# A recurrent unit's last tile worked by token halves, with one pair of weight buffers opened ahead of the unit and two high parts made by casting transfers

## The chip, the cores and the metric

The kernel runs on one core of one Trainium2 chip. The metric is the device time in microseconds (us) of one execution. The engines are named as in the profile: PE (TensorE, matrix products), DVE (VectorE), ACT (ScalarE), POOL (GpSimd) and SP (SyncE, which issues transfers). PEld is PE's loading of weights, which overlaps PE.

## The reference, cut to what matters

The program is one step of a two-layer model on 640 tokens (512 latent tokens, then 128 context tokens) of width 1024. Layer 0 is an attention layer with its feed-forward part; layer 1 is a bidirectional gated recurrent unit, then a feed-forward part. The change touches the end of layer 1's recurrent unit and the projection behind it:

```python
a = jnp.exp(log_a)
b = jnp.sqrt(-jnp.expm1(2.0 * log_a)) * (i * xc)
def step(h, ab):            # one scan per direction, forward and backward
    a_t, b_t = ab
    h = a_t * h + b_t
    return h, h
y = (hs_f + hs_b) * jax.nn.gelu(gate)
return y @ w_out, jnp.stack([hT_f, hT_b], axis=1)
# then, with one gate value per channel:
x = x + g * (y @ w_out)
# and the RMS norm of x, the modulation and the feed-forward part
```

The latent scans start from given states, the context scans from zero; the final context states are an output of their own.

## The kernel before

All data lie with the channels on the 128 partitions, in 8 tiles of channels, and the tokens along the free dimension. Every product in fp32 is made of three matmuls of rounded operands: each operand is split into a high part (a cast) and a low part (the operand minus its high part), and hi·hi, hi·lo and lo·hi are added in PSUM. So a matrix operand is not ready for PE until its cast is done, and not wholly until its subtraction is done too.

**The recurrent unit** (`lru_xr`, `lru_a`, `lru_b`, `lru_c`, `lru_gate`, `lru_d`) runs over the 8 channel tiles f, one behind the other with overlap. For each tile ACT makes sigmoids, an exponential and a square root (L1316 to L1321), DVE multiplies by the root (L1322), makes four scans (L1330: two directions, latent 512 and context 128 columns), copies the final states (L1332), adds both directions in the grid's order (L1337, L1338), multiplies by the gate (L1343), and the result y is split by L1348 (ACT, high) and L1350 (DVE, low). For the last tile, 7, the last two steps go in the two token halves of 320, (0, 320) and (320, 640).

**The projection** (`project_halves`) multiplies y (8 tiles k) by `w_out`, in 8 units f of 128 output channels, each for two token halves c0 and c1; every pair of unit and half is 24 matmuls of 320 columns, in a PSUM buffer of its own (three under the name "mm", three under "mx"). Five of them, f0c0, f0c1, f1c0, f1c1 and f2c0, start early: with k = 0 to 4, and then in turns with k = 5, 6 and 7, as the tiles of y come in. Between the turns k = 6 and k = 7 stand ten small dummy products (`keep`, L211; PE's records show twenty). Then follow f3 to f7 of c0, the sum of squares over channels of c0 (`stat`: matmuls L551 and L554, a variance on DVE L556, a power on POOL L558, a diagonal on DVE L560 and its broadcast by PE, L568), f2 to f7 of c1, and the same sum of squares for c1. A finished PSUM buffer is evicted by DVE (L598, a multiply-add on x, in two pieces where latent and context tokens meet), ACT squares the row, DVE adds the square (L537), and x goes to DRAM. The feed-forward part follows (L1168 to L1170 are its first three groups' matmuls, L1130 its product of gate and up).

**The weights** of a unit come by a transfer into `raw` (three buffers), are cast by ACT (L181) and subtracted by DVE (L183). The pairs are called whi/wlo (three buffers) or whx/wlx (three, opened with the feed-forward part's pool).

**The order.** Each engine runs its own list of instructions in order. The lists are written by a planner at build time, which runs a model of the machine; program code fixes a place only where it pins an instruction behind another (`issue_after`). So a change at one place may reorder others.

## Time and profile before

| | us |
|---|---|
| median of 3 runs (1506.61 to 1507.72) | 1506.66 |
| the profiled execution | 1508.43 |
| its span (first to last instruction) | 1506.4 |
| PE busy | 1483.1 (98%) |
| DVE busy | 1063.1 (71%) |
| ACT busy | 701.6 (47%) |
| POOL busy | 222.5 (15%) |

The busy shares are means over stages of different limits. The recurrent unit lies before about 1011 us of the span, its projection until about 1057, then the feed-forward part.

### The profile page before, as it was taken

The numbers are of one execution on the slowest core, as the hardware profiler recorded it, in microseconds if no ns is written. First come the engines' busy times: TensorE is split into PE (matmuls) and PEld (weight loads), VectorE is DVE, ScalarE is ACT, GpSimd is POOL, SyncE is SP. The second block draws the span as 40 slices with busy tenths as digits, with TensorE's granted clock in tenths as the row PEclk, the third lists the DMA queues.
The fourth block names the chain that finished last, engine by engine and source line by source line (L and its number), as shares of the span: only waits on it lengthen the run. The fifth ranks groups of instructions, "written<-read, shape, count | busy, mean of one in ns | idle before, by whom it ended". The sixth has DMA issues, their size and how long they took to land. (4 is left out here: it accounts for less than half of the span.)

```text
span 1506.4 us, 26172 instructions
## 1 busy us (share of the span) xinstructions
PE 1483.1 (98%) x10409; PEld 1435.1 (95%) x10409; DVE 1063.1 (71%) x2015; ACT 701.6 (47%) x1271; POOL 222.5 (15%) x260
## 2 busy tenths in 40 slices
PE   8999999999999999999999999999999999999997
PEld 6999999899999999999999988899999999999997
DVE  5778998679999997444443778986975665655555
ACT  4576766664332123312321569884634342524243
POOL 0112132101111110000000100000331323232311
PEclk9999999999999999999999999999999999999999
DMA  9644766446566664222222544325233131313221
GB/s 377 174 146 159 188 189 174 119 144 193 182 183 197 208 198 133 62 84 84 65 65 92 148 142 127 106 90 186 103 113 98 57 113 57 112 57 103 66 57 71
DMA packets 72330, 196.66 MB, mean 131 GB/s; under 512 B 8048, under 2 KB 24592, under 8 KB 72080
## 3 DMA queue, kind: packets, MB, share of 16 engines
q1 hardware_dynamic: 57392, 142.32, 29.9%
q0 software_dynamic: 14240, 51.98, 11.4%
q8 instruction: 82, 1.34, 0.4%
q10 hardware_dynamic: 576, 0.68, 0.1%
q14 instruction: 40, 0.33, 0.1%
HBM read 179.48 MB, written 8.92 MB: 125 GB/s over the span
## 5 line engine op out<-in xcount | busy, mean ns | idle before, releaser
L229 PE MATMUL mm<-big,whi 128*128 128x320 f32 (+3 forms) x1224 | 380.3, 311 | 1.1 <-DVE big L1350 0.9
L228 PE MATMUL mm<-big,whi 128*128 128x320 f32 (+3 forms) x1224 | 378.6, 311 | 1.5 <-ACT big L574 0.6
L230 PE MATMUL mm<-big,wlo 128*128 128x320 f32 (+3 forms) x1224 | 378.0, 310 | 0.2 <-DVE wlo L183 0.2
L228 PEld LDWEIGHTS mm<-big,whi 128*128 128x128 f32 x1224 | 229.8, 188 | 3.7 <-ACT big L574 0.9
L229 PEld LDWEIGHTS mm<-big,whi 128*128 128x128 f32 x1224 | 230.1, 188 | 3.2 <-DVE big L1350 1.5
L230 PEld LDWEIGHTS mm<-big,wlo 128*128 128x128 f32 x1224 | 230.5, 188 | 1.6 <-DVE wlo L183 0.5
L257 DVE SCALAR_TENSOR_TENSOR mprod<-mraw,csb 128x1024 f32<-128x1024 f32 x160 | 195.1, 1220 | 11.4 <-DMA mraw<-in_wm 11.0
L598 DVE SCALAR_TENSOR_TENSOR x<-mm,G,x 128x320 f32<-128x320 f32 (+2 forms) x192 | 77.7, 435 | 80.4 <-PE mm L230 80.2
L181 ACT CAST whi<-raw 128x1024 fp32r<-128x1024 f32 (+1 forms) x71 | 73.8, 1040 | 109.5 <-PE mm L229 63.4
L183 DVE TENSOR_TENSOR wlo<-raw,whi 128x1024 fp32r<-128x1024 f32 (+1 forms) x87 | 105.2, 1209 | 24.7 <-ACT whi L181 11.9
L229 PE MATMUL mm<-big,whx 128*128 128x320 f32 (+3 forms) x348 | 108.2, 311 | 0.0
L230 PE MATMUL mm<-big,wlx 128*128 128x320 f32 (+3 forms) x348 | 107.7, 310 | 0.0
L228 PE MATMUL mm<-big,whx 128*128 128x320 f32 (+3 forms) x348 | 107.6, 309 | 0.0
L253 POOL DMA_DIRECT2D mraw<-in_wm x80 | 43.1, 539 | 355.2 <-DVE mprod L257 272.2
L229 PE MATMUL mx<-big,whi 128*128 128x320 f32 (+3 forms) x281 | 87.0, 309 | 0.0
L230 PE MATMUL mx<-big,wlo 128*128 128x320 f32 (+3 forms) x281 | 86.8, 309 | 0.0
L228 PE MATMUL mx<-big,whi 128*128 128x320 f32 (+3 forms) x281 | 86.7, 309 | 0.0
L181 ACT CAST whx<-raw 128x1024 fp32r<-128x1024 f32 (+1 forms) x40 | 41.1, 1029 | 84.6 <-PE mm L229 45.7
L230 PE MATMUL mx<-big,wlx 128*128 128x320 f32 (+3 forms) x260 | 80.5, 309 | 0.0
L229 PE MATMUL mx<-big,whx 128*128 128x320 f32 (+3 forms) x260 | 80.4, 309 | 0.0
L228 PE MATMUL mx<-big,whx 128*128 128x320 f32 (+3 forms) x260 | 80.1, 308 | 0.0
L1348 ACT CAST whi<-raw 128x1024 fp32r<-128x1024 f32 (+1 forms) x41 | 41.3, 1007 | 73.2 <-PE mm L229 44.5
(363 smaller groups left out, 3710.4 us busy)
## 6 DMA issues: line engine op xcount, KB each, us to landing
raw<-in_gu SPq DMA_DIRECT2D x88, 512.0 KB, 3.5
mraw<-in_wm POOLq DMA_DIRECT2D x80, 512.0 KB, 4.0
raw<-in_dn SPq DMA_DIRECT2D x24, 512.0 KB, 3.7
sw<-in_wm SPq DMA_DIRECT2D x16, 512.0 KB, 10.7
raw<-in_wqk SPq DMA_DIRECT2D x16, 512.0 KB, 5.0
raw<-in_wi SPq DMA_DIRECT2D x16, 512.0 KB, 3.5
whi<-in_wi POOLq DMA_DIRECT2D x16, 512.0 KB, 3.9
raw<-in_dn SPq DMA_DIRECT2D x16, 448.0 KB, 3.3
```

What stands on the lines that cost most here:

```text
L181: nc.scalar.copy(hi, raw)
L183: nc.vector.tensor_tensor(lo, raw, hi.bitcast(F32), ALU.subtract)
L228: nc.tensor.matmul(ps, hi[:, k], xhi[:, k, s], start=(k == 0), stop=False)
L229: nc.tensor.matmul(ps, hi[:, k], xlo[:, k, s], start=False, stop=False)
L230: self.done = nc.tensor.matmul(ps, lo[:, k], xhi[:, k, s], start=False, stop=(k == last)).ins
L253: nc.gpsimd.dma_start(w, self.i["wm"][l * 6 + j - 2, f])
L257: nc.vector.scalar_tensor_tensor(prod, w, 1.0, self.csb[:, s], ALU.mult, ALU.mult, accum_out=out[:, s, f:f + 1])
L598: self.nc.vector.scalar_tensor_tensor(xs, ps[:, a - t0:b - t0], G[:, s, f:f + 1], xs, ALU.mult, ALU.add)
L1348: self.nc.scalar.copy(hi, v)
```

## The change

1. For tile 7 the recurrent unit's last multiply (L1322 before) is left to a new function `lru_end`, which works by parts in a written, pinned order: the latent columns' multiply, their two scans, the sums up to token 320, the gate and cast of half c0, and only then the context columns, their scans, and half c1. The copy of the final states comes last.
2. The high parts of tiles 5 and 6 are made by a casting transfer on POOL's queue, not by a cast of ACT.
3. Unit f2 of the projection takes a whx/wlx pair from a new pool `wp` that is opened ahead of the recurrent unit; its high part and that of unit f3 come by casting transfers from DRAM. So f2's low part can be made before the unit ends.
4. The turn k = 7 is divided by halves: first c0, with matmuls of f3 put between, then c1. The dummies go. f3's three parts run as all hi·hi, all hi·lo, all lo·hi.
5. The eviction of a half of the k = 7 turn is pinned behind the last subtraction of weights, and the transfer of the final states moves behind the projection in the code.

```diff
-    def unit(self, src, slot=None, after=None, nx=3):
+    def unit(self, src, slot=None, after=None, nx=3, cast=False):
...
-        if self.ptags == ["at"]:
-            nc.gpsimd.dma_start(hi, src)
+        if cast or self.ptags == ["at"]:
+            with self.pin(self.cast if after else None):
+                nc.gpsimd.dma_start(hi, src)
         else:
             nc.scalar.copy(hi, raw)
-        with self.tc.issue_after(after) if after else nullcontext():
-            nc.vector.tensor_tensor(lo, raw, hi.bitcast(F32), ALU.subtract)
+        with self.pin(after):
+            self.low = nc.vector.tensor_tensor(lo, raw, hi.bitcast(F32), ALU.subtract).ins
         return hi, lo
+
+    def wxs(self, shape, n=3):
+        if self.wp is None:
+            return [self.t(shape, F32R, v, n, self.sb) for v in ("whx", "wlx")]
+        self.nx += 1
+        n, pool = (1, self.wp) if self.nx % 3 == 1 else (2, self.sb)
+        return [self.t(shape, F32R, v, n, pool) for v in ("whx", "wlx")]
...
-        us = [self.unit(w[f], "m") for f in range(3)]
+        us = [self.unit(w[f], "mmx"[f], cast=f == 2) for f in range(3)]
...
-        turns = sorted(zip(early, pss), key=lambda e: e[0][1])
-        for k in range(KT - 3, KT):
-            if k == KT - 1:
-                self.keep(self.ps("at"), 10)
+        def turn(k, turns, pin=None):
             for (f, t0, t1), ps in turns:
                 for part in us[f]:
-                    self.done = self.nc.tensor.matmul(ps, part[:, k], hi[:, k, t0:t1], start=False, stop=False).ins
+                    with self.pin(pin):
+                        pin = self.done = self.nc.tensor.matmul(ps, part[:, k], hi[:, k, t0:t1], start=False, stop=False).ins
             for (f, t0, t1), ps in turns:
                 self.done = self.nc.tensor.matmul(ps, us[f][0][:, k], lo[:, k, t0:t1], start=False, stop=(k == KT - 1)).ins
                 if k == KT - 1:
-                    out(f, t0, t1, ps)
-        for f in range(3, KT):
-            us.append(self.unit(w[f], "mx"[f % 2]))
-            out(f, *CH[0], self.chunk(us[f], hi, lo, *CH[0]))
+                    with self.pin(self.low):
+                        out(f, t0, t1, ps)
+        sides = [[e for e in zip(early, pss) if e[0][1:] == c] for c in CH]
+        for k in range(KT - 3, KT - 1):
+            turn(k, sides[0] + sides[1])
+        us.append(self.unit(w[3], "m", ended, cast=True))
+        turn(KT - 1, sides[0])
+        t0, t1 = CH[0]
+        ps = self.ps("mx")[:, 0:HT]
+        for j, (part, v) in enumerate(((0, hi), (0, lo), (1, hi))):
+            if j == 2:
+                turn(KT - 1, sides[1], self.done)
+            for k in range(KT):
+                self.done = self.nc.tensor.matmul(ps, us[3][part][:, k], v[:, k, t0:t1], start=(j == k == 0),
+                                                  stop=(j == 2 and k == KT - 1)).ins
+        out(3, t0, t1, ps)
+        for f in range(4, KT):
+            us.append(self.unit(w[f], "xm"[f % 2]))
+            out(f, *CH[0], self.chunk(us[f], hi, lo, *CH[0], pins={0: self.done} if f == 4 else {}))
...
     def lru_d(self, f, y, G, yhi, ylo):
-        for a, b in CH if f == KT - 1 else ((0, NTOK),):
-            self.nc.vector.tensor_tensor(y[:, a:b], y[:, a:b], G[:, a:b], ALU.mult)
-            self.split(yhi[:, f, a:b], ylo[:, f, a:b], y[:, a:b])
+        self.nc.vector.tensor_tensor(y, y, G, ALU.mult)
+        hi, lo = yhi[:, f, 0:NTOK], ylo[:, f, 0:NTOK]
+        if f < KT - 3:
+            self.split(hi, lo, y)
+            return
+        self.cast = self.nc.gpsimd.dma_start(hi, y).ins
+        self.nc.vector.tensor_tensor(lo, y, hi.bitcast(F32), ALU.subtract)
+
+    def lru_end(self, f, a, h, root, G, yhi, ylo):
...
+        rooted(0)
+        for d in range(2):
+            dve(self.scan, f, a, h, d, 0)
+        for piece in ((56, 64, 0), (0, 32, 64)):
+            dve(self.directions, y, h, *piece)
+        gated(*CH[0])
+        rooted(1)
+        dve(self.scan, f, a, h, 0, 1)
+        low(*CH[0])
+        dve(self.scan, f, a, h, 1, 1)
+        dve(self.directions, y, h, 32, 56, 320)
+        dve(nc.vector.tensor_tensor, y[:, NLAT:NTOK], h[:, 0, C0:LW], h[:, 1, C0:LW], ALU.add)
+        gated(*CH[1])
+        low(*CH[1])
+        with self.pin(ins):
+            self.states(f, h)
+        return ins
...
+        wp = self.ctx.enter_context(tc.tile_pool(name="wp", bufs=1, reuse_waits="tile"))
         with self.phase("lru", at=1) as lp:
```

In `lru_end`, `rooted` is the multiply by the root, `directions` the sum of both directions for some columns of the grid, `gated` the multiply by the gate with ACT's cast behind it, `low` the subtraction; every DVE step is pinned behind the one before it.

**Where the order moves, first place.** DVE at the end of the recurrent unit, before (lt are the recurrent unit's tiles, gl the gate, big_9509 and big_9510 y's high and low part, st the states):

```order
L1350 TENSOR_TENSOR big_9510<-lt_10639,big_9509 128x640
L1322 TENSOR_TENSOR lt_10620<-lt_10620,lt_10619 128x1286
L1330 SCALAR_TENSOR_TENSOR lt_10620<-lt_10781,cols_61,lt_10620 128x512
L1330 SCALAR_TENSOR_TENSOR lt_10620<-lt_10781,lt_10620 128x128
L1330 SCALAR_TENSOR_TENSOR lt_10620<-lt_10781,cols_61,lt_10620 128x512
L1330 SCALAR_TENSOR_TENSOR lt_10620<-lt_10781,lt_10620 128x128
L1337 TENSOR_TENSOR lt_10781<-lt_10620 128x64
L1337 TENSOR_TENSOR lt_10781<-lt_10620 128x448
L1332 COPY st_74<-lt_10620 128x2
L1338 TENSOR_TENSOR lt_10781<-lt_10620 128x128
L1343 TENSOR_TENSOR lt_10781<-lt_10781,gl_10800 128x320 x2
L1350 TENSOR_TENSOR big_9510<-lt_10781,big_9509 128x320 x2
```

And DVE with the change, at the same place:

```order
L1380 TENSOR_TENSOR big_9510<-lt_10642,big_9509 128x640
L1390 TENSOR_TENSOR lt_10623<-lt_10623,lt_10622 128x2x512
L1351 SCALAR_TENSOR_TENSOR lt_10623<-lt_10784,cols_61,lt_10623 128x512 x2
L1356 TENSOR_TENSOR lt_10784<-lt_10623 128x64
L1356 TENSOR_TENSOR lt_10784<-lt_10623 128x256
L1390 TENSOR_TENSOR lt_10784<-lt_10784,gl_10802 128x320
L1390 TENSOR_TENSOR lt_10623<-lt_10623,lt_10622 128x2x128
L1351 SCALAR_TENSOR_TENSOR lt_10623<-lt_10784,lt_10623 128x128
L1390 TENSOR_TENSOR big_9510<-lt_10784,big_9509 128x320
L1351 SCALAR_TENSOR_TENSOR lt_10623<-lt_10784,lt_10623 128x128
L1356 TENSOR_TENSOR lt_10784<-lt_10623 128x192
L1390 TENSOR_TENSOR lt_10784<-lt_10623 128x128
```

The gate's multiply for the first half (128x320) stands behind two scans and two sums now, and behind four scans, three sums and the copy before.

PE at that place, before (mm and mx are PSUM buffers, whi/wlo and whx/wlx a unit's weights, at_11026 the dummies' buffer):

```order
L1054 MATMUL mx_10919<-big_9510,whi_10906 128x320
L211 MATMUL at_11026<-ident_63,ones_72 128x128 x10
L1052 MATMUL mm_10916<-big_9509,whi_10900 128x320
L1052 MATMUL mm_10916<-big_9509,wlo_10901 128x320
L1052 MATMUL mm_10918<-big_9509,whi_10906 128x320
L1052 MATMUL mm_10918<-big_9509,wlo_10907 128x320
L1052 MATMUL mm_10920<-big_9509,whi_10912 128x320
L1052 MATMUL mm_10920<-big_9509,wlo_10913 128x320
L1052 MATMUL mx_10917<-big_9509,whi_10900 128x320
```

And PE with the change (mx_11059 is unit f3's buffer):

```order
L1060 MATMUL mx_10923<-big_9510,whi_10910 128x320
L1075 MATMUL mx_11059<-big_9509,whi_11032 128x320 x7
L1058 MATMUL mm_10920<-big_9509,whi_10904 128x320
L1058 MATMUL mm_10920<-big_9509,wlo_10905 128x320
L1058 MATMUL mm_10922<-big_9509,whi_10910 128x320
L1058 MATMUL mm_10922<-big_9509,wlo_10911 128x320
L1058 MATMUL mm_10924<-big_9509,whx_10916 128x320
L1058 MATMUL mm_10924<-big_9509,wlx_10917 128x320
L1075 MATMUL mx_11059<-big_9509,whi_11032 128x320
L1075 MATMUL mx_11059<-big_9510,whi_11032 128x320 x7
L1060 MATMUL mm_10920<-big_9510,whi_10904 128x320
L1060 MATMUL mm_10922<-big_9510,whi_10910 128x320
```

Seven matmuls of f3 stand where the dummies stood, and eight more behind the six of half c0.

**Second place.** PE at the second sum of squares, before (mm_11547 is the first group of the feed-forward part, at_11491 the sums):

```order
L1168 MATMUL mm_11547<-big_10881,whx_11513 128x320
L1169 MATMUL mm_11547<-big_10881,whx_11513 128x320
L1170 MATMUL mm_11547<-big_10881,wlx_11514 128x320
L551 MATMUL at_11491<-ones_72,ssq_11049 128x128
L554 MATMUL at_11491<-ones_72,sq_11488 128x128
```

And with the change (mm_11454 is unit f7's second half, at_11484 the sums):

```order
L235 MATMUL mm_11454<-big_9509,whi_11215 128x320
L236 MATMUL mm_11454<-big_9510,whi_11215 128x320
L237 MATMUL mm_11454<-big_9509,wlo_11216 128x320
L558 MATMUL at_11484<-ones_72,ssq_11044 128x128
L561 MATMUL at_11484<-ones_72,sq_11481 128x128
```

Before, the 24 matmuls of the feed-forward part's first group (mm_11547) stood between f7's second half and the sums; with the change nothing stands between them, and that group comes behind the sums. Behind the six sums 15 matmuls of the next group and then the broadcast of the diagonal follow in both.

DVE there, before (x the residual stream, sq the squares, ssq their sum, big_10881 the feed-forward part's input, var and dg the variance and the diagonal):

```order
L1350 TENSOR_TENSOR big_10881<-x_10886,big_10881 128x320 x2
L598 SCALAR_TENSOR_TENSOR x_10886<-mx_11461,G_1335_7652,x_10886 128x192
L537 TENSOR_TENSOR ssq_11049<-ssq_11049,sq_11371 128x320
L598 SCALAR_TENSOR_TENSOR x_10886<-mx_11461,G_1335_7652,x_10886 128x128
L537 TENSOR_TENSOR ssq_11049<-ssq_11049,sq_11410 128x320
L537 TENSOR_TENSOR ssq_11049<-ssq_11049,sq_11449 128x320
L183 TENSOR_TENSOR wlx_11526<-raw_11523,whx_11525 128x1024
L183 TENSOR_TENSOR wlo_11532<-raw_11529,whi_11531 128x1024
L183 TENSOR_TENSOR wlx_11538<-raw_11535,whx_11537 128x1024
L556 TENSOR_SCALAR var_11498<-at_11491 128x3
L560 TENSOR_TENSOR dg_11502<-ident_63,rs_11500 128x384
```

And with the change:

```order
L605 SCALAR_TENSOR_TENSOR x_10890<-mm_11454,G_1335_7652,x_10890 128x192
L605 SCALAR_TENSOR_TENSOR x_10890<-mm_11454,G_1335_7652,x_10890 128x128
L544 TENSOR_TENSOR ssq_11044<-ssq_11044,sq_11364 128x320
L1424 TENSOR_TENSOR big_10885<-x_10890,big_10885 128x320 x3
L544 TENSOR_TENSOR ssq_11044<-ssq_11044,sq_11403 128x320
L544 TENSOR_TENSOR ssq_11044<-ssq_11044,sq_11442 128x320
L184 TENSOR_TENSOR wlx_11520<-raw_11517,whx_11519 128x1024
L184 TENSOR_TENSOR wlo_11526<-raw_11523,whi_11525 128x1024
L184 TENSOR_TENSOR wlx_11532<-raw_11529,whx_11531 128x1024
L563 TENSOR_SCALAR var_11491<-at_11484 128x3
L567 TENSOR_TENSOR dg_11495<-ident_63,rs_11493 128x384
```

Three subtractions of the feed-forward part's input (128x320) stand between the eviction and the last two additions now; the three subtractions of weights stand ahead of the variance in both.

## Rows read from the trace of the kernel before

**Rows 1.** the page, busy time: us, share of the span, instructions.

```profile
PE 1483.1 (98%) x10409; PEld 1435.1 (95%) x10409; DVE 1063.1 (71%) x2015; ACT 701.6 (47%) x1271; POOL 222.5 (15%) x260
```

**Rows 2.** the timeline of PE: start us, us, what, count, idle before and releaser.

```profile
1001.63 0.41 PE L230 MATMUL mm<-big,wlo 128*128 128x320 f32 x1 [0.21 <-DVE wlo L183]
...
1006.85 2.39 PE L211 MATMUL at<-ident,ones 128*128 128x128 f32 x20
1010.75 0.42 PE L1052 MATMUL mm<-big,whi 128*128 128x320 f32 x1 [1.51 <-ACT big L1348]
...
1016.71 0.30 PE L228 MATMUL mm<-big,whi 128*128 128x320 f32 x1
```

**Rows 3.** the timeline of DVE, the end of the recurrent unit.

```profile
998.20 0.82 DVE L1343 TENSOR_TENSOR lt<-lt,gl 128x640 f32<-128x640 f32 x1
...
1003.79 1.50 DVE L1322 TENSOR_TENSOR lt<-lt,lt 128x1286 f32<-128x1286 f32 x1 [0.35 <-ACT lt L1321]
1005.32 1.28 DVE L1330 TENSOR_TENSOR_SCAN lt<-lt,cols,lt 128x512 f32<-128x512 f32 x1
1006.52 0.40 DVE L1330 TENSOR_TENSOR_SCAN lt<-lt,lt 128x128 f32<-128x128 f32 x1
...
1008.33 1.21 DVE L1337 TENSOR_TENSOR lt<-lt 128x64 f32<-128x64 f32 x2
...
1009.69 0.92 DVE L1343 TENSOR_TENSOR lt<-lt,gl 128x320 f32<-128x320 f32 x2
...
1012.09 2.36 DVE L183 TENSOR_TENSOR wlx<-raw,whx 128x1024 fp32r<-128x1024 f32 x2 [0.46 <-ACT whx L181]
1014.71 1.01 DVE L598 SCALAR_TENSOR_TENSOR x<-mm,G,x 128x320 f32<-128x320 f32 x2 [0.26 <-issue]
```

**Rows 4.** the timeline of ACT, the same stretch.

```profile
1002.48 1.27 ACT L1321 ACTIVATE lt<-lt 128x1286 f32<-128x1286 f32 x1
...
1010.24 0.86 ACT L1348 CAST big<-lt 128x320 fp32r<-128x320 f32 x2 [4.43 <-DVE lt L1343]
```

**Rows 5.** the DMA view: tensors, queue, count, KB each, median us to landing.

```profile
whi<-in_wi POOLq DMA_DIRECT2D x16, 512.0 KB, 3.9
...
KS<-KS POOLq DMA_DIRECT2D x4, 240.0 KB, 5.7
...
out_nh<-st POOLq DMA_DIRECT2D x1, 8.0 KB, 1.7
```

**Rows 6.** the timeline of PE around the second sum of squares.

```profile
1053.78 0.31 PE L230 MATMUL mx<-big,wlx 128*128 128x320 f32 x1
1053.93 0.31 PE L1168 MATMUL mm<-big,whx 128*128 128x320 f32 x1
...
1057.44 0.38 PE L551 MATMUL at<-ones,ssq 128*128 128x128 f32 x2
...
1061.41 0.80 PE L568 MATMUL mx<-dg,ones 128*128 128x128 f32 x5 [0.27 <-DVE dg L560]
```

**Rows 7.** the timeline of DVE, the same stretch.

```profile
1052.56 0.90 DVE L1350 TENSOR_TENSOR big<-x,big 128x320 fp32r<-128x320 f32 x2
1054.13 0.42 DVE L598 SCALAR_TENSOR_TENSOR x<-mx,G,x 128x192 f32<-128x192 f32 x1 [0.68 <-PE mx L230]
...
1055.12 1.08 DVE L537 TENSOR_TENSOR ssq<-ssq,sq 128x320 f32<-128x320 f32 x2
```

**Rows 8.** the timeline of PE in the feed-forward part.

```profile
1093.26 0.41 PE L1168 MATMUL mm<-xt,whx 128*128 128x320 f32 x1 [1.46 <-DVE g L1130]
```

**Rows 9.** stretches: busy us and count of PE, PEld, DVE, ACT, POOL; PEclk; DMA.

```profile
1004.00:1013.00 9.00, 7.49 (x56) 7.30 (x55) 8.38 (x14) 4.55 (x6) 0.56 (x1) 1.00 0.16 52
1499.00:1500.00 1.00, 0.00 (x0) 0.00 (x0) 1.00 (x3) 0.31 (x1) 0.65 (x1) 1.00 0.19 68
1500.00:1501.00 1.00, 0.00 (x0) 0.00 (x0) 1.00 (x2) 0.95 (x2) 0.00 (x0) 1.00 0.20 69
1502.00:1503.00 1.00, 0.00 (x0) 0.00 (x0) 0.00 (x0) 0.00 (x0) 0.00 (x0) 0.50 1.04 402
```

More of the change, by code (lines that the diff above doesn't have):

```diff
@@ L37 @@
 C0 = 515
+LATPR = (slice(0, 512), slice(C0, LW))
 FG = (1, 1, 1)
@@ L1321, in lru_b, with scan @@
         self.turn(AF.Sqrt, lambda: nc.scalar.activation(tr, tr, AF.Sqrt, scale=0.25))
+        if f == KT - 1:
+            return a, ti, tr
         nc.vector.tensor_tensor(ti, ti, tr, ALU.mult)
         return a, ti
+    def scan(self, f, a, h, d, part):
+        init = 0.0 if part else self.col(f"h{d}", f)
+        hv, av = [t[:, d, LATPR[part]] if d == 0 else t[:, d, LATPR[part]][:, ::-1] for t in (h, a)]
+        return self.nc.vector.tensor_tensor_scan(hv, av, hv, init, ALU.mult, ALU.add)
@@ new lines, in directions, with states @@
+    def directions(self, y, h, c0, c1, q0):
+        fn, bn = [h[:, d, 0:NLAT].rearrange("p (r c) -> p c r", r=ROWS) for d in range(2)]
+        yv = y[:, q0:q0 + (c1 - c0) * ROWS].rearrange("p (c r) -> p c r", r=ROWS)
+        return self.nc.vector.tensor_tensor(yv, fn[:, c0:c1], bn[:, c0:c1], ALU.add)
+    def states(self, f, h):
+        ends = bass.AP(tensor=h.tensor, offset=h[:, 0, LW - 1:LW].offset, ap=[list(h.ap[0]), [C0 + 1, 2]])
+        return self.nc.vector.tensor_copy(self.st.rearrange("p (d k) -> p k d", d=2)[:, f], ends)
@@ L1333, in lru_c @@
-        y = a[:, 0, 0:NTOK]
-        fn, bn = [h[:, d, 0:NLAT].rearrange("p (r c) -> p c r", r=ROWS) for d in range(2)]
-        for c0, c1, q0 in ((56, 64, 0), (0, 56, 64)):
-            yv = y[:, q0:q0 + (c1 - c0) * ROWS].rearrange("p (c r) -> p c r", r=ROWS)
-            nc.vector.tensor_tensor(yv, fn[:, c0:c1], bn[:, c0:c1], ALU.add)
-        nc.vector.tensor_tensor(y[:, NLAT:NTOK], h[:, 0, C0:LW], h[:, 1, C0:LW], ALU.add)
+            for part in range(2):
+                self.scan(f, a, h, d, part)
@@ new lines, in lru_d, with dve, rooted, gated @@
+        hi, lo = yhi[:, f, 0:NTOK], ylo[:, f, 0:NTOK]
[5 more added lines that the diff above has]
+    def lru_end(self, f, a, h, root, G, yhi, ylo):
+        nc = self.nc
+        y = a[:, 0, 0:NTOK]
+        ins = None
+        def dve(step, *args):
+            nonlocal ins
+            with self.pin(ins):
+                ins = step(*args).ins
+        def rooted(part):
+            v = h[:, :, LATPR[part]]
+            dve(nc.vector.tensor_tensor, v, v, root[:, :, LATPR[part]], ALU.mult)
+        def gated(t0, t1):
+            dve(nc.vector.tensor_tensor, y[:, t0:t1], y[:, t0:t1], G[:, t0:t1], ALU.mult)
+            nc.scalar.copy(yhi[:, f, t0:t1], y[:, t0:t1])
+        def low(t0, t1):
+            dve(nc.vector.tensor_tensor, ylo[:, f, t0:t1], y[:, t0:t1], yhi[:, f, t0:t1].bitcast(F32), ALU.subtract)
+        rooted(0)
[12 more added lines that the diff above has]
+        low(*CH[1])
+        with self.pin(ins):
+            self.states(f, h)
+        return ins
```

32 lines of the change are left out of this document (15 added, 17 removed).

## The prediction

> **What bounds the kernel now.** I read the page's busy table first: TensorE (PE) is busy for 1483.1 of 1506.4 us [rows 1]. Only some 23 us can be won at all, and a change elsewhere moves the end only by filling a gap of PE or opening one. PE's instructions around the end of the recurrent unit come next [rows 2]: after 1006.85 it runs twenty dummy matmuls, then idles 1.51 us for the scalar engine's (ACT) cast of the last high part, so nothing useful starts before 1010.75. VectorE (DVE) is the engine behind that wait: from 1003.79 on it works without a gap through tile 7's multiply, scans, sums and gate [rows 3], and ACT's cast sits idle 4.43 us for it [rows 4]. Two places further on carry the rest of the sum: the second sum of squares, where PE and DVE are in step [rows 6, 7], and a PE idle of 1.46 us at 1093.26, where DVE is behind [rows 8].
>
> **The end of the recurrent unit.** Call T0 the start of tile 7's multiply on DVE: 1003.79 before, released by ACT's square root, which starts at 1002.48 and takes 1.27 [rows 3, 4]. The change takes two 640-column casts and one weight cast off ACT in front of it, some 2 us of work by the 0.86 that two 320-column ones take [rows 4], so ACT no longer decides. What decides now is the casting transfer of tile 6: its product ends at 999.02 (998.20 + 0.82), then comes the transfer, then DVE's subtraction of 0.82 [rows 3]. No SBUF-to-SBUF cast is in the trace. Nearest rows: a cast of a 512 KB weight on the same queue takes 3.9 us, a 240 KB copy inside SBUF 5.7, an 8 KB store 1.7 [rows 5]. On the line from 1.7 at 8 KB to 3.9 at 512 KB, 320 KB would take 3.1; I take 3.4, between that and the weight's 3.9, which is the row most like it. T0 = 999.02 + 0.1 for the issue + 3.4 + 0.8 = 1003.3. The ends, 1.7 and 5.7, give 1001.6 and 1005.6.
>
> The Trainium skill (DMA: Bandwidth & Descriptors, "Anatomy of one DMA — SWDGE (gpsimd) path") has a fixed cost of about 2.0 us plus bytes over 436 GB/s on this queue; an estimate from that page is 2.75 us for these 320 KB. The rows stand above it: for 512 KB it would give 3.2 where the trace has 3.9 [rows 5], so I stay with the rows; by the page T0 would be 0.65 earlier and the sum below 0.65 smaller.
>
> From T0 to the first half's high part before: DVE reaches the gate at 1009.69, 5.90 after T0, and PE starts 1.06 later [rows 2, 3]. Now only four fifths of the multiply (1.2), two of the four scans (1.20 each, by 1005.32 to 1006.52) and 320 of 512 columns of the two sums (1.21 for all in the rows; I take 0.95) stand ahead: 1.2 + 2.4 + 0.95 + 1.06, about 5.7 instead of 6.96. PE would start at 1009.0. It is free earlier: the dummies (2.39) go, and so does the hold-up of some 0.46 at 1001.63 (0.21 idle, the rest slower starts), because unit 2's low part is made before the unit. It arrives at 1006.4, does seven matmuls of unit 3 (0.146 each, by 1053.78 to 1053.93 [rows 6]) and waits 1.6.
>
> What is late next: DVE. The pinned chain runs to about T0 + 9.0 (ctx multiply, two short scans, sums, gate, two subtractions), and behind it stand three 1024-column subtractions, some 1.15 apart (two took 2.36 at 1012.09 [rows 3]), and only then the first eviction. So unit 3's low part is there at T0 + 10.15, and PE, which does 18 and 6 matmuls from T0 + 5.85, stands there from T0 + 9.4: 0.8 idle. Eight matmuls on, the next unit needs a PSUM buffer whose eviction (half of the 1.01 for two, from T0 + 12.4) ends at T0 + 12.87: 1.5 idle. That unit starts at 1003.3 + 12.87 = 1016.2; before, the same amount of work was done at 1016.71 [rows 2]. **First term: -0.5 us.** Of the 3.9 us of dummies and idle almost all comes back as three waits on DVE. With the bounds of T0 the term is -2.2 to +1.8. The early weight pair costs nothing that I can see: its transfer waits for nothing late on POOL's queue, and its subtraction (1.22) falls on DVE ahead of a tile's multiply, where DVE waits for ACT; without that cover it would push T0 by up to 1.2.
>
> **The second sum of squares.** Here the order on PE moves, by itself, as a consequence of the other allotment of PSUM buffers and weights. Before, unit 7's second half ended with the matmul at 1053.78, then 24 matmuls of the feed-forward part ran, and the six sums started at 1057.44 [rows 6]. DVE needed until 1056.20 for eviction and squares (1054.13, then 1055.12 + 1.08 [rows 7]), all under those 24. Now the sums stand directly behind the last matmul. Eviction starts 0.35 after that matmul's start (1054.13 - 1053.78); its two pieces and one addition take 0.99 (to 1055.12); three 320-column subtractions now stand ahead of the last two additions (0.4 each, as two take 0.90 with their overlap, 1.2 in all [rows 7]), and these take 1.08. With 0.1 to PE that is 3.7 us from start to start, where 0.15 would be the pitch. **Second term: +3.5 us.** It would be at least 2.3 if the three subtractions fitted in ahead, and none of it can be hidden, since PE's queue is in order.
>
> Behind it, unchanged, DVE has three 1024-column subtractions before the variance, so the diagonal that PE needs comes 5.2 us after the last addition, as before (1056.20 to 1061.41). PE has in that time, as before, six sums and 15 matmuls (1057.44 to 1061.41, 0.27 of it idle, 0.43 with the last matmul's pitch: 3.5 us), but it now begins them 0.1 behind the addition and not 1.24 later. So 1.6 are left idle, where 0.43 were. **Third term: +1.1 us.** That the first sum's broadcast comes 19 matmuls later in PE's list changes the order only.
>
> **What is given back.** At 1093.26 PE waits 1.46 us for a product of DVE, which has been working without a break [rows 8]. DVE passes the second sum only about 0.5 later than before, and one more subtraction (0.4) stands ahead of that product; PE comes 4.1 later than before (-0.5 + 3.5 + 1.1). So the product is ready 1.7 us ahead of PE. **Fourth term: -1.5 us.** From there the kernel is PE's again, and I move nothing in the rest.
>
> Sum: -0.5 + 3.5 + 1.1 - 1.5 = +2.6 us. The profiled execution was 1508.43 us (span 1506.4); it would become 1511.0. The median of the runs is 1506.66, 1.77 under the profiled one; the difference carried over gives **1509.3 us**. What the measurement can tell from no change is 0.2%, 3.0 us: 1503.65 to 1509.67. So I forecast no change, on the slow side of it.
>
> **The rivals.**
> *The clock falls in the new idle (slower).* Through the idle of 1.51 us the granted clock stayed at 1.00, that is 2.4 GHz (the stretch 1004 to 1013 [rows 9]). At the kernel's end no matmul runs from 1499 on; the clock was still 1.00 in the stretch 1500 to 1501 and 0.50, 1.2 GHz, in 1502 to 1503 [rows 9]. An idle of 3.4 us ahead of the second sum lies between the two. At half clock the six sums and the 15 matmuls behind it would take 3.5 us longer; the diagonal's wait of 1.6 hides part, so some 1.9 us are added: 1511.2. Against it: the fall would have to come within the idle and last. It decides from an idle that reaches the fall; a landing of the tile 6 cast at 5.7 us adds 2.3 in the same direction (1511.6).
> The Trainium skill (TensorE: Matmul & The Clock Gate, Part 1) says that the array's default is the throttled clock and that activity alone releases it; the trace agrees at the kernel's end, and no row shows it in the middle.
> *The idle at the second sum is smaller, or wholly paid by the product (same).* If the subtractions fit ahead of the eviction, and T0 comes at 1002.6, the second term is 2.3 and the first -1.2: 0.7 in all, and 1507.4. For it: before, DVE idled 0.68 ahead of the eviction [rows 7]. Against it: DVE now begins this stretch behind eight modulations and has no slack that I can count.
> *The gain stays (faster).* PE is free at 1006.4 and does useful work where it ran dummies and idled for 3.9 us. If the evictions don't stand behind DVE's subtractions, and the six sums find their squares done, nothing is given back: 1506.66 - 3.9 = 1502.8. With the second sum's wait at 2.3 it is 1505.1, which is no longer faster. For it: the gap itself is in the rows. Against it: the subtractions' places in DVE's queue are fixed.
> *The change doesn't take effect*: excluded, as the order on the engines has moved.
>
> **How the numbers follow.** Forecast 0.55, with its own range 1508.0 to 1510.6 (0.4 either way for the transfer, some 0.9 for the two chains on DVE), of which a third lies above 1509.67: same 0.36, slower 0.19. Clock or late landing 0.20, all slower. Smaller idle, or a gain kept in part (1505.1), 0.15, all same. The gain stays 0.10, all faster. Together faster 0.10, same 0.51, slower 0.39. The range 1505.8 to 1511.6 reaches from between the two cheaper cases, 1505.1 and 1507.4, to the late landing.
>
> **What would show it.** In the profile after: tile 7's multiply between 1002.5 and 1004; the first matmul with tile 7's high part about 5.7 behind it; no dummies; an eviction wait of about 1.5 us at the unit after unit 3, near 1016; an idle of about 3.4 us ahead of the second sum's matmuls, released by DVE's addition; about 1.6 ahead of the diagonal's; none at the product near 1095. I am wrong if the six sums find their squares done, if the first halves don't wait for DVE, or if the wait at the product stays.

## The result, and the profile after

The changed kernel takes 1510.2 us (median of 13 runs, 1509.8 to 1512.0), the kernel before 1507.4 in the same comparison (13 runs, 1506.6 to 1507.9). The ratio is 1.0021, with an interval of 1.0013 to 1.0030: 2.8 us longer, at the edge of what a measurement can tell. Forecast were 2.6 us more and 1509.3. The profiled span went from 1506.4 to 1508.8.

PE's timeline after, at the end of the recurrent unit (start us, us, what, count, idle ahead and its releaser), is the answer to [rows 2]:

```profile
1006.22 1.18 PE L1075 MATMUL mx<-big,whi 128*128 128x320 f32 x7
1008.18 0.41 PE L1058 MATMUL mm<-big,whi 128*128 128x320 f32 x1 [0.78 <-ACT big L1398]
...
1012.60 1.44 PE L1075 MATMUL mx<-big,wlo 128*128 128x320 f32 x8 [0.59 <-DVE wlo L184]
...
1015.42 0.38 PE L235 MATMUL mm<-big,whi 128*128 128x320 f32 x1 [1.38 <-DVE x L605]
```

The dummies are gone and so is the idle of 1.51; in their place stand three waits, 0.78, 0.59 and 1.38. The unit behind f3 starts at 1015.42, before at 1016.71 [rows 2]. The two executions are compared from a matmul far ahead of the change, the first that waits for ACT's copy into xr, the recurrent unit's input: it started at 855.98 before and starts at 855.87 after. From there 1.18 us are won here.

DVE's timeline of the same stretch stands against [rows 3]:

```profile
1001.67 0.83 DVE L1380 TENSOR_TENSOR big<-lt,big 128x640 fp32r<-128x640 f32 x1 [0.73 <-DMA big<-lt]
1002.41 1.22 DVE L1390 TENSOR_TENSOR lt<-lt,lt 128x1024 f32<-128x1024 f32 x1
1003.67 2.46 DVE L1351 TENSOR_TENSOR_SCAN lt<-lt,cols,lt 128x512 f32<-128x512 f32 x2
...
1007.14 0.49 DVE L1390 TENSOR_TENSOR lt<-lt,gl 128x320 f32<-128x320 f32 x1
...
1011.32 1.22 DVE L184 TENSOR_TENSOR wlo<-raw,whi 128x1024 fp32r<-128x1024 f32 x1
...
1013.59 1.22 DVE L184 TENSOR_TENSOR wlo<-raw,whi 128x1024 fp32r<-128x1024 f32 x1
1014.73 1.00 DVE L605 SCALAR_TENSOR_TENSOR x<-mm,G,x 128x320 f32<-128x320 f32 x2
```

Tile 7's multiply starts at 1002.41, behind the subtraction that waits for the casting transfer; the three weight subtractions stand ahead of the first eviction, as forecast. The transfers, as the view of DMA issues has them (tensors, queue, count, KB each, median us to landing), belong to [rows 5]:

```profile
big<-lt POOLq DMA_DIRECT2D x2, 320.0 KB, 2.5
whx<-in_wlo POOLq DMA_DIRECT2D x1, 512.0 KB, 3.8
whi<-in_wlo POOLq DMA_DIRECT2D x1, 512.0 KB, 4.4
```

At the second sum of squares, PE after, against [rows 6]:

```profile
1052.48 0.31 PE L237 MATMUL mm<-big,wlo 128*128 128x320 f32 x1
1056.60 0.46 PE L558 MATMUL at<-ones,ssq 128*128 128x128 f32 x2 [3.81 <-DVE ssq L544]
...
1059.20 0.47 PE L1189 MATMUL mm<-big,whi 128*128 128x320 f32 x1
1059.47 0.47 PE L1190 MATMUL mm<-big,whi 128*128 128x320 f32 x1
...
1061.63 0.31 PE L1191 MATMUL mm<-big,wlo 128*128 128x320 f32 x1
1061.78 0.83 PE L575 MATMUL mx<-dg,ones 128*128 128x128 f32 x6
1062.37 0.39 PE L1189 MATMUL mx<-big,whx 128*128 128x320 f32 x1
```

The sums stand straight behind the projection's last matmul and wait 3.81 us. The group that ran ahead of them before, at 1053.93 with whx in a buffer "mm" [rows 6], now runs behind the diagonal's broadcast, at 1062.37, in a buffer "mx". Behind the sums the matmuls come 0.27 apart, not 0.15, until 1060.80, and PE does not wait for the diagonal at 1061.78. The stretches (busy us and count of PE, PEld, DVE, ACT, POOL; PEclk; DMA) say why:

```profile
1053.00:1057.00 4.00, 0.40 (x3) 0.43 (x4) 3.54 (x9) 2.56 (x6) 0.00 (x0) 1.00 0.13 47
1057.00:1058.00 1.00, 1.00 (x10) 1.00 (x9) 1.00 (x2) 0.00 (x0) 0.00 (x0) 0.79 0.00 0
1058.00:1061.00 3.00, 3.00 (x13) 3.00 (x13) 1.97 (x4) 0.00 (x0) 0.85 (x1) 0.50 0.78 232
1061.00:1062.00 1.00, 1.00 (x9) 1.00 (x8) 0.52 (x1) 0.93 (x1) 0.00 (x0) 1.00 0.88 311
```

After the idle the granted clock (the last column but two) is 0.79, then 0.50, that is 1.2 GHz, for three us. DVE's timeline of that stretch, against [rows 7]:

```profile
1052.83 0.68 DVE L605 SCALAR_TENSOR_TENSOR x<-mm,G,x 128x192 f32<-128x192 f32 x2 [0.28 <-PE mm L237]
1053.42 0.48 DVE L544 TENSOR_TENSOR ssq<-ssq,sq 128x320 f32<-128x320 f32 x1
1053.82 1.29 DVE L1424 TENSOR_TENSOR big<-x,big 128x320 fp32r<-128x320 f32 x3
...
1055.96 0.49 DVE L544 TENSOR_TENSOR ssq<-ssq,sq 128x320 f32<-128x320 f32 x1 [0.46 <-DVE ssq L544]
...
1060.96 0.56 DVE L567 TENSOR_TENSOR dg<-ident,rs 128x384 f32<-128x384 f32 x1 [1.03 <-POOL rs L565]
```

The three subtractions stand between the additions, and the last addition waits 0.46 more: its square on ACT had to wait for a buffer that the addition before it frees.

In the feed-forward part, against [rows 8], and further on:

```profile
1092.87 0.41 PE L1189 MATMUL mm<-xt,whi 128*128 128x320 f32 x1 [0.77 <-ACT g L1197]
...
1234.55 0.41 PE L236 MATMUL mm<-big,whi 128*128 128x320 f32 x1 [0.20 <-DVE big L1424]
...
1235.62 0.41 PE L1132 MATMUL mx<-xt,wuh 128*128 128x320 f32 x1 [0.50 <-ACT snap L1138]
```

The wait of 1.46, which DVE's product ended, has become one of 0.77 that ACT ends. Before, three more waits followed; of the same kind only the 0.20 and 0.50 above are left after:

```profile
1175.74 0.41 PE L1111 MATMUL mx<-xt,wuh 128*128 128x320 f32 x1 [0.45 <-ACT snap L1117]
...
1232.32 0.41 PE L229 MATMUL mm<-big,whi 128*128 128x320 f32 x1 [0.36 <-DVE big L1350]
1233.47 0.41 PE L1111 MATMUL mx<-xt,wuh 128*128 128x320 f32 x1 [0.59 <-ACT snap L1117]
```

### The profile page after: what moved, and what is told of

It is laid out like the page before. It is cut to its first block, busy times and chain, and to the rows that moved or that the text cites. A ratio compares the mean times of both kernels' runs of the same rounds, so it can differ in the third digit from the quotient of the medians.

```text
span 1508.8 us, 26147 instructions
## 1 busy us (share of the span) xinstructions
PE 1482.4 (98%) x10389; PEld 1434.3 (95%) x10389; DVE 1061.8 (70%) x2017; ACT 698.1 (46%) x1267; POOL 229.3 (15%) x264
## 5 line engine op out<-in xcount | busy, mean ns | idle before, releaser
L605 DVE SCALAR_TENSOR_TENSOR x<-mm,G,x 128x128 f32<-128x128 f32 (+2 forms) x193 | 77.8, 434 | 78.1 <-PE mm L237 78.1
L236 PE MATMUL mm<-big,whx 128*128 128x320 f32 (+3 forms) x357 | 110.9, 311 | 0.0
L235 PE MATMUL mm<-big,whx 128*128 128x320 f32 (+3 forms) x357 | 110.2, 309 | 0.0
L236 PE MATMUL mx<-big,whx 128*128 128x320 f32 (+3 forms) x248 | 76.8, 310 | 0.0
L237 PE MATMUL mx<-big,wlx 128*128 128x320 f32 (+3 forms) x248 | 76.8, 310 | 0.0
L235 PE MATMUL mx<-big,whx 128*128 128x320 f32 (+3 forms) x248 | 76.5, 308 | 0.0
```

The lines of the kernel that those rows point to most:

```text
L235: nc.tensor.matmul(ps, hi[:, k], xhi[:, k, s], start=(k == 0), stop=False)
L236: nc.tensor.matmul(ps, hi[:, k], xlo[:, k, s], start=False, stop=False)
L237: self.done = nc.tensor.matmul(ps, lo[:, k], xhi[:, k, s], start=False, stop=(k == last)).ins
L605: self.nc.vector.scalar_tensor_tensor(xs, ps[:, a - t0:b - t0], G[:, s, f:f + 1], xs, ALU.mult, ALU.add)
```

## The experiments

PSUM buffers are handed out by a counter, `ng`, which `pg()` advances: it picks "mm" or "mx" by its place in a pattern. f3 of the projection was written anew and takes an "mx" buffer directly, so the counter does not advance there and all later groups shift by one place. The first feed-forward group thereby falls on an "mx" buffer, a ring that the sum's broadcast uses too and had claimed first, and in PE's list it stands behind that broadcast. That is **theory A**: the loss at the second sum is that one place in a counter, and the slow clock behind the idle costs nothing, because PE would else have waited for the diagonal. That the shared ring is why the group moves is read from the program; the experiments test the counter, not the ring. The rivals: the new end of the recurrent unit makes the loss, and not the counter (**theory B**), or the slow clock is a cost by itself (**theory C**). **Theory D** came with experiments 5 to 7: the wait for the product g comes from DVE working beside POOL's weight sums (L1110 after), and it brings a fall of the clock that costs nearly as much again. **Theory E**, in experiment 8: the diagonal's wait is the place of the weight subtractions in DVE's order. In the expectation of experiment 4 the letters D and E name two other readings, of that experiment alone.

To compare executions I count from the start of that matmul behind ACT's copy into xr (855.98 before): what comes ahead of it is the same in all kernels and varied by up to 2.2 us among these executions. "To wuh" is the time from there to the first feed-forward matmul with the weights wuh, "to the end" that to the last norm's broadcast (1489.20 before). These two columns are of one execution each; the ratios are of all runs.

| kernel | median, us | ratio to before (95%) | to wuh | to the end |
|---|---|---|---|---|
| before | 1507.4 to 1507.8 | 1 | 277.75 | 633.22 |
| changed | 1510.2 | 1.0021 (1.0013, 1.0030) | 280.99 | 635.79 |
| 1 changed, counter advanced | 1508.8 | 1.0003 (0.9994, 1.0012) | 280.44 | 634.49 |
| 2 before, counter not advanced | 1511.2 | 1.0029 (1.0018, 1.0040) | 283.74 | 639.40 |
| 3 changed, dummies in the idle | 1510.9 | 1.0021 (1.0011, 1.0030) | 281.68 | 636.46 |
| 4 as 1, casts on ACT | 1508.2 | 1.0003 (0.9994, 1.0011) | 279.02 | 633.16 |
| 5 as 1, dummies ahead of g | 1508.9 | 1.0010 (1.0001, 1.0019) | 279.66 | 634.21 |
| 6 as 1, sums later | 1506.2 | 0.9993 (0.9984, 1.0002) | 277.77 | 631.49 |
| 7 before, sums later | 1506.1 | 0.9988 (0.9979, 0.9997) | 275.91 | 629.94 |
| 8 as 6, low parts later | 1505.1 | 0.9983 (0.9974, 0.9992) | 275.95 | 629.50 |
| 9 changed, sums later | 1510.4 | 1.0017 (1.0008, 1.0026) | 280.11 | 634.41 |
| 10 as 7, low parts later | 1505.7 | 0.9987 (0.9978, 0.9996) | 276.93 | 631.81 |

**1. The counter advanced at f3.**

```diff
+        self.ng += 1
         ps = self.ps("mx")[:, 0:HT]
```

> The changed kernel with one line more: the counter that picks a PSUM buffer's name (mm or mx) is advanced by one for unit f3, as it was before the change, so that every later product gets the same kind of buffer as before. On PE the first group of the feed-forward part then stands ahead of the second sum of squares again. Theory A (the order at the second sum moved because the first group fell on an mx buffer, whose ring also holds the sum's broadcast): the idle of 3.81 us ahead of the sums goes (under 0.3 us is left), the clock stays at 1.00 there, the wait of about 1.4 us at the product near 1093 comes back, and the time is 0.5 to 1.5 us under the kernel before (about 1506.3 where before is 1507.4). Theory B (DVE, with its pinned chain, is simply late at the second sum): an idle of over 2 us stays and the time is 1509 or more.

Measured: 1508.8, ratio 1.0003. PE of this kernel, around the second sum and at the product:

```profile
1056.62 0.38 PE L558 MATMUL at<-ones,ssq 128*128 128x128 f32 x2
...
1061.60 0.91 PE L575 MATMUL mx<-dg,ones 128*128 128x128 f32 x6 [1.29 <-DVE dg L567]
...
1094.08 0.42 PE L1190 MATMUL mm<-xt,whx 128*128 128x320 f32 x1 [2.09 <-DVE g L1152]
```

The old order is back, the idle of 3.81 is gone, and the clock is 1.00 through the sums. So the order part of theory A holds. The expected gain over the kernel before did not come: PE reaches the sums 0.5 earlier than before (200.96 from the start against 201.46), but the diagonal makes it wait 1.29 where it waited 0.27, and the product 2.09 where it waited 1.46. Behind the wait of 2.09 the clock falls (stretches of this kernel, same columns):

```profile
1092.00:1094.00 2.00, 0.00 (x0) 0.00 (x0) 2.00 (x4) 0.00 (x0) 0.14 (x1) 1.00 0.55 210
1094.00:1096.00 2.00, 1.92 (x9) 1.92 (x10) 2.00 (x5) 1.94 (x4) 0.00 (x0) 0.70 0.00 0
1096.00:1098.00 2.00, 2.00 (x10) 2.00 (x9) 2.00 (x3) 0.98 (x2) 0.00 (x0) 0.50 0.53 144
```

**2. The kernel before with f3 taken out of the counter**, and nothing else of the change.

```diff
-        for f in range(3, KT):
+        us.append(self.unit(w[3], "x"))
+        ps = self.ps("mx")[:, 0:HT]
+        self.some(us[3], hi, lo, *CH[0], ps, range(KT))
+        out(3, *CH[0], ps)
+        for f in range(4, KT):
```

> The kernel before with nothing changed but that counter: unit f3 takes its mx buffer without advancing it, as in the change. Theory A: the group falls behind the sums here too, an idle of 3 to 4 us stands ahead of the second sum, and the time is 3 to 5 us over the kernel before (about 1511.4). Theory B: the order at the second sum costs nothing without the new end of the recurrent unit; the time is within 1 us of the kernel before.

Measured: 1511.2, ratio 1.0029, that is 3.5 us over the kernel before by the medians. The kernel before, untouched in its recurrent unit, now waits ahead of its sums, somewhat less than the 3 to 4 us expected:

```profile
1056.35 0.46 PE L551 MATMUL at<-ones,ssq 128*128 128x128 f32 x2 [2.67 <-DVE ssq L537]
```

So the counter alone makes the idle and a loss of that size, and theory B falls. The profiled execution was a long one of this kernel (1513.9), so its two columns above overstate the loss.

**3. Dummy products in the idle**, so that the clock stays up.

```diff
-            self.stat(t0, t1)
+            self.stat(t0, t1, 12 if c else 0)
```

> The changed kernel with 12 dummy products (24 records) on PE ahead of the second sum of squares, where it idles 3.81 us; they read constants and end before the squares are ready. Theory A (the fall of the clock behind the idle cost almost nothing, since PE would have waited for the diagonal anyway): the clock stays at 1.00, an idle of 1.3 to 1.8 us appears ahead of the diagonal's broadcast, and the time is within 0.5 us of the changed kernel (1510.2 where before is 1507.4). Theory C (the fall costs its whole 1.7 us): the time is about 1508.5.

Measured: 1510.9, the ratio of the changed kernel. PE and the clock of this kernel:

```profile
1057.27 0.49 PE L558 MATMUL at<-ones,ssq 128*128 128x128 f32 x2 [1.07 <-DVE ssq L544]
...
1062.42 0.91 PE L575 MATMUL mx<-dg,ones 128*128 128x128 f32 x6 [1.35 <-DVE dg L567]
```

```profile
1058.00:1060.00 2.00, 2.00 (x17) 2.00 (x17) 2.00 (x3) 0.00 (x0) 0.00 (x0) 1.00 0.31 59
```

The clock is 1.00, and PE now waits 1.35 for the diagonal, which comes as late as it did (205.94 from the start, 205.91 in the changed kernel). The slow clock at the second sum cost nothing: it filled a wait. Theory C falls for this place.

**4. The casts of tiles 5 and 6 by ACT again**, with the counter advanced.

```diff
...
-        if f < KT - 3:
+        if f < KT - 1:
             self.split(hi, lo, y)
```

> The first experiment's kernel (counter restored), with the high parts of tiles 5 and 6 cast by ACT again and not by transfers. Theory D (what the change gains at the end of the recurrent unit comes from an earlier start of tile 7's multiply alone, since everything behind it runs at a fixed distance on DVE): the multiply starts at about 1003.7 and not at 1002.4, the unit behind f3 starts 1.2 to 1.4 us later, and the time is 0.8 to 1.5 us over the first experiment, that is within 0.5 us of the kernel before. Theory E (the halves' order carries the gain): the time stays within 0.4 us of the first experiment.

Measured: 1508.2, ratio 1.0003, as without it. With no casting transfer left to stand behind, f3's transfer also goes out earlier. Tile 7's multiply starts 0.2 later from the common start than in experiment 1 (1004.41 - 857.58 = 146.83 against 1002.30 - 855.66 = 146.64), where 1.3 was expected, and the unit behind f3 0.2 later (159.85 against 159.66). So the casting transfers are worth some 0.2 us at that place, and nothing that the time shows. Most of what the multiply gained stays: it is still 0.98 earlier than before (1003.79 - 855.98 = 147.81). In this run ACT's list ahead of tile 7's square root has both tile casts again; it lacks one weight cast, which took 1.04 us at 996.96 before. So most of the gain at that multiply goes with that cast; no run takes it apart alone.

**5. Dummy products in the wait for g**, with the counter advanced.

```diff
...
+                if c and n == 4:
+                    self.keep(self.ps("at"), 8)
...
-                    nc.tensor.matmul(ps, lo[:, k], xh, start=False, stop=(k == KT - 1))
+                    self.done = nc.tensor.matmul(ps, lo[:, k], xh, start=False, stop=(k == KT - 1)).ins
```

(`self.done` is the matmul that the dummies are pinned behind.)

> The changed kernel with the count of groups advanced at f3, and with 8 dummy products on TensorE in the idle ahead of the product that waits for the first feed-forward tile's product g (2.09 us at 1094.08 with the count alone, after which the granted clock was 0.70, 0.50, 0.94 in three stretches of 2 us). Theory D (that wait costs twice: 0.63 us more than before's 1.46, and some 1.5 us of slow clock behind it): the clock stays at 1.00 there, the stretch from the second diagonal to the first wuh product falls from 74.5 to about 73 us, and the time is about 1507.3, within 0.5 of the kernel before. Rival (the slow stretch only fills waits that come later anyway): the time stays at 1508.5 to 1509.

Measured: 1508.9. The clock stays at 1.00 in the three stretches of experiment 1's rows, and from the second diagonal to the first matmul with wuh it takes 72.39 us, 74.50 without the dummies: the place went as theory D has it. The time did not: in the profiled execution PE waited 1.67 us for a weight cast at 1024.49, ahead of the dummies, where experiment 1 waited 0.32, which takes 1.3 of the gain, but the median of 11 runs shows no gain either. What the fall of the clock behind g costs in time stays open.

**6. POOL's weight sums behind the third subtraction of t4**, with the counter advanced.

```diff
...
-        self.pw = t4 if k < 2 else self.pw
+        self.pw = t4
```

> The changed kernel with the count advanced, and GpSimd's weight sums pinned behind the third subtraction of t4 in place of the second one. Theory D (VectorE's steps near 1080 to 1092 take two to three times as long while GpSimd forms these sums, so that g comes 2.09 us late): with the sums later the wait for g and the fall of the clock behind it go, 2.1 + 1.5 = 3.6 us less than with the count alone, about 1505 (0.998 of before). Rival (the sums are needed as soon, and their wait only moves to the first products that use them): within 0.7 of the count alone, 1508 to 1509.5.

Measured: 1506.2, ratio 0.9993; against experiment 1 that is 2.6 us less, where 3.6 were expected. PE has no wait left between the second diagonal and the first matmul with wuh, 70.60 us instead of 74.50. DVE's timeline in experiment 1 and in this kernel shows where it comes from:

```profile
1083.12 4.18 DVE L1425 TENSOR_TENSOR big<-x,big 128x320 fp32r<-128x320 f32 x3
1087.22 3.09 DVE L1031 TENSOR_TENSOR c<-x 128x320 f32<-128x320 f32 x2
...
1093.55 0.48 DVE L1152 TENSOR_TENSOR g<-mm,g 128x320 f32<-128x320 f32 x1
```

```profile
1085.93 1.97 DVE L1425 TENSOR_TENSOR big<-x,big 128x320 fp32r<-128x320 f32 x3
1087.83 0.88 DVE L1031 TENSOR_TENSOR c<-x 128x320 f32<-128x320 f32 x2
...
1091.22 0.48 DVE L1152 TENSOR_TENSOR g<-mm,g 128x320 f32<-128x320 f32 x1
```

The same five subtractions take 7.27 us beside POOL's sums and 2.85 where the sums start later, at 1089.41. A smaller part is order: the low part of the sums' own weights (wlx<-sum, 1.89 us) stood ahead of the product in experiment 1 and comes behind it here.

The profiled execution, the longest of the 11 runs (1508.3), also lost time at another place: behind the three waits at the end of the recurrent unit (1.13, 0.58 and 1.38 here) the clock fell, and the first unit behind them took 5.13 us, where the same unit takes 3.59 in experiment 1. Little of these 1.5 us was hidden by a later wait: PE reaches the second diagonal 1.2 later than in experiment 1 (207.17 against 205.94) and still waits 1.27 for it. The granted clock (last column but two):

```profile
1018.00:1021.00 3.00, 3.00 (x13) 3.00 (x13) 2.90 (x9) 1.81 (x5) 0.00 (x0) 0.50 1.04 414
```

**7. The kernel before with the later sums alone** (the same line).

> The kernel before with only the later pin of GpSimd's weight sums. Theory D: its 1.46-us wait for the product at 1093.26 goes, and nothing else changes: 1.5 us less, about 1506.2 (0.999). Rival (the wait moves to the sums' users): no change, within 0.5 of before.

Measured: 1506.1, ratio 0.9988, where 1506.2 was expected. The wait of 1.46 is gone (70.60 us for that stretch as well), and it did not move to the users of the sums.

**8. As 6, with the units' low parts later on DVE.**

```diff
...
-self.unit(self.i["gu"][l, c * NF + f], None, self.sq if f else None)
+self.unit(self.i["gu"][l, c * NF + f], None, (None, None, self.sq, self.var, self.dg, self.dg)[2 * f + c])
```

> The same as the changed kernel with the count advanced and the later pin of the sums, and with the subtractions of the units' low parts on VectorE pinned behind the variance and the diagonal of the second normalization, so that these two steps stand ahead of them. Theory E (with the count alone the diagonal's wait of 1.29 us is VectorE's order: one subtraction of 1.22 us ahead of the variance): the wait goes, 1.3 us less than the later pin alone, about 1504. Rival (the weights' low parts are then late for the units behind the sum): the wait moves to the unit's third products, and the time is that of the later pin alone or up to 1 us more.

Measured: 1505.1, ratio 0.9983, the lowest of all kernels here; 1504 was expected. PE's wait for the diagonal:

```profile
1061.17 0.91 PE L575 MATMUL mx<-dg,ones 128*128 128x128 f32 x6 [0.58 <-DVE dg L567]
```

It fell from 1.27 in experiment 6 to 0.58 and did not go: a subtraction of 1.21 still begins between the variance and the diagonal. Theory E holds for half of it. By the medians the edit is worth 1.1 us against experiment 6, with intervals that overlap.

**9. The changed kernel with the later sums alone**, the counter as the change has it.

> The changed kernel as it stands (groups not counted at f3) with only the later pin of GpSimd's weight sums. If the wait of 0.77 us for g at 1092.87 and what is left of later waits (0.20 at 1234.55, 0.50 at 1235.62) come from VectorE beside the sums, they go: 0.8 to 1.5 us less than the changed kernel, about 1509, while the 3.8-us idle ahead of the second sum of squares stays. Against the later pin with the count advanced (1506.2) it is then 2.5 to 3 us slower: that is the price of the shifted count when no later wait hides it. Rival (the price of the shifted count is itself hidden by other waits): within 0.7 of 1506.2.

Measured: 1510.4. The waits for g are gone; the idle ahead of the sums is not:

```profile
1058.63 0.46 PE L558 MATMUL at<-ones,ssq 128*128 128x128 f32 x2 [3.82 <-DVE ssq L544]
```

Against experiment 6, which differs in the counter alone, it is 4.2 us longer by the medians and 2.9 by the profiled executions (634.41 against 631.49), of which experiment 6 had lost 1.5 to the slow clock told there. The ratios' intervals are apart. So the place in the counter costs about 4 us where no later wait pays for it. Where the waits for g stand behind it, it costs less: the changed kernel is 1.4 us longer than experiment 1. The expected gain over the changed kernel, 0.8 to 1.5, shows in its profiled execution (1.4) and not in its median.

**10. The kernel before with both later pins.**

> The kernel before with the later pin of GpSimd's weight sums and the later pins of the units' low parts, the same two edits that bring the changed kernel with the count advanced to 1505.1. If the change by itself is worth its 1.1 us at the end of the recurrent unit once nothing behind takes it back, this runs about 1 us longer, 1506.1, the same as with the later sums alone (before's diagonal waits only 0.43 us, so the second edit gains at most that). Rival (the change's gain is lost all the same, in the first feed-forward groups or in the transfers): within 0.4 of 1505.1.

Measured: 1505.7, ratio 0.9987 against 0.9983 in experiment 8. The intervals overlap for most of their width, so this does not tell whether the change, with its counter set right and these two edits around it, is worth a microsecond. In the profiled executions experiment 8 is 1.0 ahead at the second diagonal (205.35 against 206.33), but the second edit seems to hurt the kernel before: its diagonal came at 205.31 in experiment 7, with a wait of 0.27, and waits 0.58 here. Against experiment 7 no more than 0.4 is left to the last norm's broadcast (629.50 against 629.94).

## Why the prediction was right

The forecast of no change on the slow side, with 2.6 us more, came out at 2.8 more. The mechanism was right in its main terms: the idle at the second sum, the waits on DVE and the return at the product all came where they were said to. That the sum came so close is partly luck: the gain of the first term came out at more than double and that of the fourth at half, and the misses went in opposite directions. Measured by PE's starts in the two profiled executions:

- **First term, forecast -0.5, measured -1.2.** The structure was right: no dummies, and three waits of 0.78, 0.59 and 1.38 where 1.6, 0.8 and 1.5 were forecast. What was mis-sized is the casting transfer: 3.4 us were taken, from the rows of a weight's cast out of DRAM, and it took 2.5 inside SBUF; with its issue, DVE's subtraction starts 2.87 behind the product's end (998.80 to 1001.67) and not 3.5. The Trainium skill (DMA: Bandwidth & Descriptors, "Anatomy of one DMA — SWDGE (gpsimd) path") gave an estimate of 2.75, so there the page was nearer than the rows I preferred, while for the 512 KB weights, 3.8 and 4.4 in the trace, its 3.2 is too short. T0 came 0.9 earlier than forecast (0.2 of it because the product itself ended earlier), just outside the 1002.5 to 1004 that was said to show it, and 0.7 of it reached PE. Experiment 4 adds that casts on ACT would have given nearly the same T0.
- **Second term, forecast +3.5, measured +4.0.** Counted as the forecast counts it, from start to start less a pitch of 0.15, it is 1056.60 - 1052.48 - 0.15; 3.81 of it is shown as idle. It stands where it was said to stand, released by DVE's addition. The difference is about the 0.46 that the last addition waited for its square's buffer, which the sum had not seen. The forecast gave as reason the allotment of PSUM buffers; experiments 1 and 2 narrow it to one place of a counter.
- **Third term, forecast +1.1, measured +1.1.** From 1.18 ahead at the unit behind f3, PE is 0.48 behind at the second diagonal, with 24 matmuls still to do that before had done; these take 3.4 (74.04 us from the diagonal to the first matmul with wuh in experiment 9, 70.60 in experiments 6 to 8, none with a wait for g). In all that is 5.1, of which 4.0 is the second term. The way was another: no idle stands ahead of the diagonal, as the slow clock filled it.
- **The rival of the clock.** Its mechanism came: the clock fell to 0.50 in the new idle. Its price of 1.9 did not come: the slow matmuls used up the diagonal's wait and ended with it (no idle at 1061.78). The rival counted 21 matmuls at half clock, but the clock fell only behind the first four of the six sums, and was back at 1.00 before the diagonal. Experiment 3 shows the price to be nil.
- **Fourth term, forecast -1.5, measured -0.7.** The wait for DVE's product went as said, but another wait, of 0.77, stands at the same place. By the names in the rows PE waits there for a PSUM buffer "mm" that an older group filled, until that group's reader is done. Which group that is follows the counter: where it is advanced (before, experiments 1 and 4) the wait ends with DVE's product, where it is not (the changed kernel, experiments 2 and 3) with ACT's activation g. ACT's list after has the cast of POOL's weight sums ahead of that activation, and the cast waits for POOL:

```profile
1091.43 1.05 ACT L1422 CAST whx<-sum 128x1024 fp32r<-128x1024 f32 x1 [3.71 <-POOL sum L1110]
1092.38 0.43 ACT L1197 ACTIVATE g<-mm 128x320 f32<-128x320 f32 x1
```

With the sums later (experiment 9) the activation runs ahead of that cast and the wait is gone. The forecast looked at DVE's product only, though it had seen that the buffers were allotted otherwise. This is the term that failed most, and of its sign of being wrong, a wait that stays at the product, half came.
- **"I move nothing in the rest"** was wrong by 0.7 to the good: three later waits (0.45, 0.36 and 0.59) became two, of 0.20 and 0.50. Why is not shown. PE comes later to them, but in experiment 7, where it comes 1.8 earlier than before, only one of 0.24 is left.

Sum of the measured terms: -1.2 + 4.0 + 1.1 - 0.7 - 0.7 = +2.5; the two profiled executions, from the common start to the last norm's broadcast, differ by 635.79 - 633.22 = 2.57.

The rival "the gain stays" spoke of 1502.8. With the order set right (experiment 1) it does not stay: at the sums only 0.5 us are left of it, and the diagonal and the product, both DVE's, take them back.

## What to carry to other kernels

A buffer taken past the counter that hands out buffers shifts every later group; look for that first when a planner's order moves at a place that the edit does not touch. An idle made on the engine that bounds the kernel, or a slow clock behind it, costs what no later wait gives back: the place in the counter cost 1.4 us where waits stood behind it and about 4 where none did, and a slow clock cost nothing ahead of the diagonal's wait and 1.2 us in experiment 6. Look for what PE waits for next before adding a price. And where DVE or ACT is behind, see first which of POOL's work runs beside it or is waited for in its list; starting that work later was worth more here than the change.

## What the runs showed of the hardware

- DVE's subtractions with two inputs in SBUF take 4.18 us for three beside POOL's sums (experiment 1), and 1.29 for three in the changed kernel's stretch from 1084.00, where POOL is the one held up: two of its steps take 7.80 us, while one takes 1.01 at 1088.44 in experiment 6. The Trainium skill (SBUF — State Buffer, "Who interferes with whom") says that a DVE instruction with two SBUF inputs contends with a GpSimd instruction that reads SBUF; the trace agrees, in both directions.

```profile
1084.00 1.29 DVE L1424 TENSOR_TENSOR big<-x,big 128x320 fp32r<-128x320 f32 x3
```

```profile
1079.07 7.80 POOL L1033 TENSOR_TENSOR x<-x,c 128x320 f32<-128x320 f32 x2 [18.15 <-ACT big L1422]
```

- The granted clock fell to 0.50 behind idles of 3.81 us (the changed kernel), 2.67 and 2.04 us (experiment 2) and 2.09 us (experiment 1), and stayed at 1.00 through and behind the 1.51 of [rows 2, 9] and the 1.35 of experiment 3. The last idle does not decide it alone: at the end of the recurrent unit it fell behind waits of 1.13, 0.58 and 1.38 in experiment 6, and stayed at 1.00 behind 0.85, 0.58 and 1.38 in experiment 9. In the changed kernel it was back at 1.00 in the stretch 1061 to 1062, where PE had resumed at 1056.60.
- A casting transfer of 320 KB inside SBUF took 2.5 us, less than the 3.8 and 4.4 of the 512 KB that come from DRAM on the same queue.
